# A gate pair's products in another order, and three moves of work in a hybrid state-space and attention block

## The chip, the cores and the metric

The kernel runs on one core of a Trainium2 chip. The metric is the device time of one execution in microseconds (us); a time of a kernel is the median of several executions. A profile is one more execution, recorded by the hardware profiler.

## What is computed

One block with 1024 frames and 1024 channels. An RMS norm of the input is modulated by a scale and a shift that come from a vector c, and one wide product of the result with `w_in` gives eight pieces:

```
mod = c @ w_ada[l] + b_ada[l]
shift, scale, gate = jnp.split(mod, 3, axis=-1)
h = _rmsnorm(x, g_pre[l]) * (1.0 + scale[:, None]) + shift[:, None]
proj = h @ w_in[l]
u_s, z_s, q_lat, kv_lat, k_rope, z_m, gl_s, gl_m = jnp.split(proj, split_at, axis=-1)
y_s = _ssm_branch(u_s, ...)          # 64 groups of 16 channels, 64 complex states each, a scan over frames
glu_a, glu_b = jnp.split(jax.nn.gelu(y_s) @ w_glu[l] + b_glu[l], 2, axis=-1)
y_s = ((glu_a * jax.nn.sigmoid(glu_b)) * jax.nn.silu(z_s)) @ w_br_ssm[l]
y_m = _mla_branch(q_lat, kv_lat, k_rope, ...)   # latent attention, 16 heads, rotary key
y_m = (y_m * jax.nn.silu(z_m)) @ w_br_mla[l]
merged = jax.nn.sigmoid(gl_s) * y_s + jax.nn.sigmoid(gl_m) * y_m
out = merged @ w_out[l]
x = x + gate[:, None] * _rmsnorm(out, g_post[l])
```

The four gates `z_s, z_m, gl_s, gl_m` are 32 tiles of 128 channels by 1024 frames.

## The kernel before

**Engines.** PE does the matrix products, DVE and POOL the elementwise work, ACT copies and functions, SP issues most of the transfers. Every engine runs its own instructions in one fixed order. For the part that the change touches, the code is written step by step and a scheduler sets each engine's order when the program is built, by its own estimate of times; the last part of the kernel is ordered by hand and isn't touched.

**Exact products.** A 32-bit product is made of three fast ones. A weight tile is split in halves of four blocks: ACT rounds it (`whi`, L113) and DVE subtracts (`wlo`, L114); four such pairs of buffers exist. A product over four blocks is 12 matmuls of 128x512.

**Head.** DVE makes the modulation in four quarters, `m` (L259 for the first of eight steps, L261 for seven more). PE sums a quarter (`mp`, L290) and transposes the normed input (`xtp`, L303), ACT makes `h`, and PE then makes the first three pieces u0 to u2 (`up`, L323). Beside that, DVE works on the layer's parameters: `exact_exp` for `dt` and `mag`, the angle `th`, the tables of powers and rotations (`rot`), all on small tiles. They go out to tables in DRAM, `tab_d` and `rot_d`, from which the state-space part reads.

**State-space blocks.** Eight blocks of two half blocks, numbered 0 to 15. For a half block, `ssm_wt` makes weights (`wt`, L809 to L811), `ssm_win` transposes them (`wps`, L819), and `ssm_turns` makes a table of turns: DVE computes `w` (L878 to L883), ACT writes it to `pk`, and four transfers bring it to `cs` (L891). `cs` and `pk` have one buffer each. `ssm_states` makes the inputs on PE (`xps`, L900) and the states on DVE (`z`, L915 to L922; L919 is the scan). `ssm_taps` makes `kps` on PE (L847), `kt` on ACT and DVE (L850), sends it through DRAM and back into `tt` by four transfers (L855). `ssm_y` needs `tt` and `z` (`yps`, L931).

**Gates.** In between, `next_gate(n)` hands out n units of other work for PE: first u3 to u7, then five plain tiles for the latents (four units each), then gate products, one unit each. `PER_SLOT` says how many at the three places of a block. Two gate tiles are a pair; its four quarters of outputs come from seven products by a scheme of Strassen and Winograd, each 12 matmuls. Their sums are made in `after` by DVE: five into `u` and the gate tiles `ga`, `gb` (L567, L605, L607, L612) and one more; `ga` and `gb` then go through ACT. Twelve pairs run in this way, four are deferred in part.

**Buffers.** Products land in PSUM tiles called `gp_`, each for two products (0 and 1, 2 and 3, 4 and 5, 6 alone); three such tiles exist. A tile is free when the last sum that reads it is done. Sums live in five buffers "ev" of 128x1024 that the whole part shares.

Of the kernel before, what the change touches and what calls it, by code (L numbers as in the profile page):

```python
# [8 lines left out]
F32 = mybir.dt.float32  # L9
# [17 lines left out]
NH = 16  # L27
L = 8

PER_SLOT = (5, 5, 4) * 8  # L30
AHEAD = 2
LAG = 4
ASIDE = 3
# [38 lines left out]
def _body(ctx, tc, a, out):  # L72
# [178 lines left out]
    def mod_quarter(n):  # L251

        m0 = xp.tile([128, 512], F32, name=f"m0{n}")
        for k in range(KT):
            wm = xp.tile([128, 512], F32, tag="wm", name="wm", bufs=8)
            wm_dma = nc.sync.dma_start(out=wm, in_=a["w_mod"][n, k])
            ck = cols[:, C_C + k:C_C + k + 1]
            if k == 0:
                V.tensor_scalar(m0, wm, ck, None, op0=ALU.mult)  # L259
            else:  # L260
                V.scalar_tensor_tensor(m0, wm, ck, m0, op0=ALU.mult, op1=ALU.add)  # L261
        macc.append(m0)
        return wm_dma

    for q in range(2):
        for t in range(4 * q, 4 * q + 4):
# [8 lines left out]
                V.tensor_scalar(xt[t], xt[t], r, None, op0=ALU.mult)  # L275
    first_w = []
    for n in range(4):
        wm_dma = mod_quarter(n)
        if n < 3:
            first_w.append(load_raw(a["w_in"][n]))  # L280
            if n < 2:
                first_w[n] = split_w(first_w[n])
# [65 lines left out]
    nc.sync.dma_start(out=dcol, in_=a["s_d"])  # L348
    lr, li = par[:, 1, :], par[:, 2, :]
    dt = tp.tile(GN, F32, name="dt")  # L350
    exact_exp(tp, dt, par[:, 0, :], GN, "dt")
    mag = tp.tile(GN, F32, name="mag")
    th = tp.tile(GN, F32, name="th")
    V.tensor_tensor(th, lr, dt, op=ALU.mult)
    exact_exp(tp, mag, th, GN, "mag")
    V.tensor_tensor(th, li, dt, op=ALU.mult)
    reduce_angle(tp, th, GN, "th")
    sn = tp.tile(GN, F32, name="sn")
    cs = tp.tile(GN, F32, name="cs")
    sin_cos(tp, sn, cs, th, GN, "th")  # L360

    pr = tp.tile([128, 9, G], F32, name="pr")
    pi = tp.tile([128, 9, G], F32, name="pi")
# [65 lines left out]
    fi = tp.tile(GN, F32, name="fi")  # L429
    den = tp.tile(GN, F32, name="den")  # L430
    nr = tp.tile(GN, F32, name="nr")
    V.tensor_tensor(den, lr, lr, op=ALU.mult)
    V.tensor_tensor(fr, li, li, op=ALU.mult)
    V.tensor_tensor(den, den, fr, op=ALU.add)
    V.reciprocal(den, den)
    V.tensor_scalar(nr, pr[:, 1, :], 1.0, None, op0=ALU.subtract)
    V.tensor_tensor(fr, nr, lr, op=ALU.mult)
    V.tensor_tensor(fi, pi[:, 1, :], li, op=ALU.mult)
# [114 lines left out]
    def gate_pair(p):  # L553
# [21 lines left out]
        def left(n):  # L575
            if n == 0:
                t["a"], t["b"] = load_raw(a["w_in"][8 + 2 * p]), load_raw(a["w_in"][9 + 2 * p])
                t["s"] = xp2.tile([128, KT, 128], F32, tag="sx", name="sx")
            a1, a2, b1, b2 = t["a"][:, 0:4], t["a"][:, 4:8], t["b"][:, 0:4], t["b"][:, 4:8]
            s1, s2 = t["s"][:, 0:4], t["s"][:, 4:8]  # L580
            if n == 0:
                P.tensor_tensor(s1, b1, b2, op=ALU.add)  # L582
                P.tensor_tensor(s2, s1, a1, op=ALU.subtract)
            if n == 2:
                P.tensor_tensor(a2, a2, s2, op=ALU.subtract)
            if n == 3:
                P.tensor_tensor(a1, a1, b1, op=ALU.subtract)
            return split_half((a1, a2, s2, s1, a2, a1, b2)[n])

        def product(n, w):  # L590
            if n % 2 == 0:
                t["p"] = ps.tile([128, S], F32, tag="A", name="gp_")
            t[n] = t["p"][:, HALF[n % 2]]
            quad_product(t[n], w, (0, 1, 2, 3, 5, 4, 6)[n])

        def after(n):
            if n == 0:
                t["u"], t["ga"] = ev("u"), ev("ga")
                A.activation(t["u"][:, HALF[0]], t[0], AF.Copy)
                return  # L600
            u1, u2 = t["u"][:, HALF[0]], t["u"][:, HALF[1]]
            if n == 1:
                add((t["ga"], 0), t[1], u1)
            elif n == 2:
                V.tensor_tensor(u2, t[2], u1, op=ALU.add)  # L605
            elif n == 3:
                V.tensor_tensor(u1, t[3], u2, op=ALU.add)  # L607
            elif n == 4:
                add((t["ga"], 1), t[4], u1)
                out_(t["ga"], p % 4 * 2)  # L610
            elif n == 5:
                V.tensor_tensor(u2, t[5], u2, op=ALU.add)  # L612
                t["gb"] = ev("gb")
                add((t["gb"], 1), t[3], u2)
            else:
                add((t["gb"], 0), t[6], u2)
                out_(t["gb"], p % 4 * 2 + 1)

        return left, product, after
# [124 lines left out]
    pos = tp.tile([128, 8], I32, name="pos")  # L744
    nc.sync.dma_start(out=pos, in_=a["pos"])
    posf = tp.tile([128, 8], F32, name="posf")
    V.tensor_copy(posf, pos)
    RS = [128, 8, 16]
    ang = tp.tile(RS, F32, name="ang")
    V.tensor_tensor(ang, posf.unsqueeze(2).to_broadcast(RS),  # L750
# [186 lines left out]
    u = ssm_load(0)  # L937
    wt = ssm_wt(0)
    turns = ssm_turns(0)
    next_gate(4)  # L940
    z = [ssm_states(0, ssm_win(wt), u[0], turns)]
    turns = ssm_turns(1)
    z.append(ssm_states(1, ssm_win(ssm_wt(1)), u[1], turns))
    turns = ssm_turns(2)
    ca = [ssm_ca(q) for q in range(2)]
    next_gate(4)
# [5 lines left out]
    for b in range(NB):  # L952
# [7 lines left out]
        spread()  # L960
        if more:
            z.append(ssm_states(2 * b + 2, ssm_win(wt), u[0], turns))
            wt = ssm_wt(2 * b + 3)
        spread()
        ssm_y(b, *this)
        if more:
            turns = ssm_turns(2 * b + 3)
            z.append(ssm_states(2 * b + 3, ssm_win(wt), u[1], turns))
            ca = [ssm_ca(2 * b + 2 + q) for q in range(2)]
            if b + 2 < NB:  # L970
                turns = ssm_turns(2 * b + 4)
# [993 lines left out]
```

## Time and profile before

| | |
|---|---|
| median of 3 executions | 1526.53 us (1525.48 to 1528.39) |
| the profiled execution | 1522.02 us, span 1520.2 us, mean granted clock 0.948 |
| head, to the end of the modulation sums | 0 to 60.9 us |
| u0 to u2 and on, tables made | 60.9 to 131 us |
| first five half blocks (z of half block 4 starts at its end) | 131 to 249.3 us |
| half blocks 4 to 14 (z to z) with gate pairs | 249.3 to 521 us |
| the last half blocks, to the operand of the latents' norm (`knrbdg`, L173) | 521 to 587 us |
| rotary, attention, output | 587 to 1520 us |

The stages overlap; the borders are single events read from the timeline. In rows of the timeline a figure in square brackets is idle time of that engine just before the instruction, with what ended it; x2 and so on is a count. A wait that the page calls "issue" was for nothing that the profile shows. The clock of PE is given as a share of 2.4 GHz.

### The profile page before, as it was taken

The numbers are of one execution on the slowest core, as the hardware profiler recorded it, in microseconds if no ns is written. First come the engines' busy times: TensorE is split into PE (matmuls) and PEld (weight loads), VectorE is DVE, ScalarE is ACT, GpSimd is POOL, SyncE is SP. The second block draws the span as 40 slices with busy tenths as digits, with TensorE's granted clock in tenths as the row PEclk, the third lists the DMA queues.
The fourth block names the chain that finished last, engine by engine and source line by source line (L and its number), as shares of the span: only waits on it lengthen the run. The fifth ranks groups of instructions, "written<-read, shape, count | busy, mean of one in ns | idle before, by whom it ended". The sixth has DMA issues, their size and how long they took to land. (4 is left out here: it accounts for less than half of the span.)

```text
span 1520.2 us, 19089 instructions
## 1 busy us (share of the span) xinstructions
PE 1335.6 (88%) x6172; PEld 1079.7 (71%) x6172; DVE 1203.1 (79%) x1917; ACT 765.6 (50%) x1374; POOL 595.9 (39%) x438
## 2 busy tenths in 40 slices
PE   3898988789889989977997999988999989989796
PEld 2686776668667767756876788866777767868574
DVE  5984799888989976896776877678777788787877
ACT  6522344344434334443756677756644465645553
POOL 1430564222423233453454434426033725556232
PEclk9899999899999999988998999989999999999999
DMA  8588555346435538674323321142278747873522
GB/s 321 208 156 215 177 167 174 108 127 180 132 121 154 149 108 282 229 268 144 114 85 139 115 64 53 36 118 84 81 221 263 234 146 277 289 264 122 188 72 97
DMA packets 154132, 246.34 MB, mean 162 GB/s; under 512 B 49824, under 2 KB 89632, under 8 KB 153520
## 3 DMA queue, kind: packets, MB, share of 16 engines
q1 hardware_dynamic: 147408, 224.14, 47.2%
q10 hardware_dynamic: 6336, 19.93, 3.4%
q8 instruction: 49, 0.80, 0.2%
q0 software_dynamic: 288, 1.05, 0.2%
q14 instruction: 51, 0.42, 0.1%
HBM read 161.97 MB, written 74.65 MB: 156 GB/s over the span
## 5 line engine op out<-in xcount | busy, mean ns | idle before, releaser
L1426 DVE TENSOR_TENSOR wlo<-lr,whi 128x512 fp32r<-128x512 f32 x137 | 93.9, 685 | 70.1 <-ACT lr L1423 69.8
L1196 POOL TENSOR_TENSOR plo<-p,phi 128x512 fp32r<-128x512 f32 x65 | 85.3, 1320 | 154.6 <-ACT phi L1194 119.2
L1188 ACT ACTIVATE p<-s_ps 128x512 f32<-128x512 f32 (+1 forms) x192 | 92.2, 488 | 64.2 <-DVE plo L1196 38.3
L114 DVE TENSOR_TENSOR wlo<-wraw,whi 128x512 fp32r<-128x512 f32 x110 | 97.0, 886 | 34.4 <-ACT whi L113 34.3
L113 ACT ACTIVATE whi<-wraw 128x512 fp32r<-128x512 f32 x110 | 68.3, 627 | 89.6 <-POOL wraw L667 11.2
L1196 DVE TENSOR_TENSOR plo<-p,phi 128x512 fp32r<-128x512 f32 (+3 forms) x127 | 81.0, 648 | 30.8 <-ACT phi L1194 30.2
L1194 ACT ACTIVATE phi<-p 128x512 fp32r<-128x512 f32 (+1 forms) x192 | 98.8, 525 | 4.1
L1538 PE MATMUL sw<-ge_hi,wlo 128*128 128x512 f32 x224 | 89.8, 401 | 6.7 <-DVE wlo L1426 6.7
L1538 PE MATMUL sw<-ge_hi,whi 128*128 128x512 f32 x224 | 88.5, 395 | 0.9 <-ACT oe L1213 0.7
L1538 PE MATMUL sw<-ge_lo,whi 128*128 128x512 f32 x224 | 88.2, 394 | 0.0
L1184 PE MATMUL s_ps<-q_hi,k_hi 128*128 128x512 f32 (+1 forms) x192 | 71.3, 372 | 12.8 <-DMA q_hi<-mr 11.0
L1419 ACT ACTIVATE whi<-raw 128x512 fp32r<-128x512 f32 x80 | 50.3, 629 | 61.5 <-PE sw L1538 42.5
L1211 PE MATMUL o_ps<-phi,v_hi 128*128 128x512 f32 (+1 forms) x192 | 69.4, 361 | 9.3 <-ACT phi L1194 9.1
L1211 PE MATMUL o_ps<-plo,v_hi 128*128 128x512 f32 (+1 forms) x192 | 66.9, 367 | 6.1 <-DVE plo L1196 5.1
L1184 PE MATMUL s_ps<-q_lo,k_hi 128*128 128x512 f32 (+1 forms) x192 | 69.1, 360 | 0.0
L1184 PE MATMUL s_ps<-q_hi,k_lo 128*128 128x512 f32 (+1 forms) x192 | 69.0, 360 | 0.0
L1211 PE MATMUL o_ps<-phi,v_lo 128*128 128x512 f32 (+1 forms) x192 | 67.6, 353 | 0.0
L1414 POOL TENSOR_TENSOR raw<-raw 128x512 f32<-128x512 f32 x16 | 22.8, 1427 | 102.9 <-DVE S L1409 60.8
L582 POOL TENSOR_TENSOR sx<-wraw 128x512 f32<-128x512 f32 x12 | 16.3, 1362 | 115.5 <-DMA wraw<-in_w_in 115.5
L1538 PEld LDWEIGHTS sw<-ge_hi,wlo 128*128 128x128 f32 x224 | 42.0, 188 | 21.8 <-DVE wlo L1426 12.5
L810 POOL TENSOR_TENSOR tm<-tab 128x512 f32<-128x512 f32 x16 | 22.6, 1414 | 87.2 <-DVE z L917 27.9
L1184 PEld LDWEIGHTS s_ps<-q_hi,k_hi 128*128 128x128 f32 x192 | 37.7, 196 | 21.1 <-issue 12.9
(1977 smaller groups left out, 4548.9 us busy)
## 6 DMA issues: line engine op xcount, KB each, us to landing
wraw<-in_w_in SPq DMA_DIRECT2D x53, 512.0 KB
wm<-in_w_mod SPq DMA_DIRECT2D x32, 256.0 KB
cs<-pk SPq DMA_DIRECT2D x64, 128.0 KB
raw<-in_w_glu SPq DMA_DIRECT2D x14, 512.0 KB
hq<-h_d SPq DMA_DIRECT2D x12, 512.0 KB
xt<-in_x SPq DMA_DIRECT2D x8, 512.0 KB
h_d<-hk SPq DMA_DIRECT2D x8, 512.0 KB
u_d<-ue SPq DMA_DIRECT2D x8, 512.0 KB
```

The source lines that it names most:

```text
L113: A.activation(hi, raw, AF.Copy)
L114: eng.tensor_tensor(lo, raw, hi.bitcast(F32), op=ALU.subtract)
L810: P.tensor_tensor(tm[:, :, 0:8, :], wi_.unsqueeze(3).to_broadcast(bc), bs_.unsqueeze(2).to_broadcast(bc), op=ALU.mult)
L1184: T.matmul(s_ps[:, 0:w], l[t][:, ks], r[t][:, qs:c1], start=(j == 0), stop=(j == 2))
L1188: lp["exp"] = A.activation(p32[:, o:w], s_ps[:, o:w], AF.Exp, scale=SCALE)
L1194: A.activation(phi[:, o:w], p32[:, o:w], AF.Copy)
L1196: eng.tensor_tensor(plo[:, o:w], p32[:, o:w], phi[:, o:w].bitcast(F32), op=ALU.subtract)
L1211: T.matmul(o_ps[half][:, c0:c0 + w], l[sl][:, kt, vs], r[:, 0:w], start=(kt == 0 and j == 0), stop=(last and j == 2))
L1414: P.tensor_tensor(src[4], a1, b1, op=ALU.subtract)
L1419: A.activation(hi, src[j], AF.Copy)
L1426: V.tensor_tensor(lo, x, hi.bitcast(F32), op=ALU.subtract)
L1538: T.matmul(p_, l[:, k, :], r[:, k, :], start=(k == 0 and i == 0), stop=(k == 3 and i == 2))
```

## The change

Four edits. (1) In a gate pair, the quarter products 3 and 4 of the scheme change places, so that `a1` less `b1` is the left side of the fourth product and `s1` of the fifth. The second sum of the products' tile 2 and 3 is then made after product 3, and `gb` is written for the first time after product 4 instead of 5. The number of splits, products and sums is the same. (2) The parameter steps on DVE (`exact_exp` twice, the angle, sine and cosine, `den`, `posf`) may only be issued after the last step of the modulation. (3) In the loop, `ssm_turns` of the odd half block is called ahead of its `ssm_wt` and not after `ssm_y`; ahead of the loop `ssm_wt(1)` gets its own line. (4) Eight units of other work ahead of the first half block's states where there were four, four more ahead of the second's, and one unit less in each of the eight blocks; the sum of units is the same.

```diff
-PER_SLOT = (5, 5, 4) * 8
+PER_SLOT = (5, 4, 4) * 8
...
-                V.scalar_tensor_tensor(m0, wm, ck, m0, op0=ALU.mult, op1=ALU.add)
+                last_m = V.scalar_tensor_tensor(m0, wm, ck, m0, op0=ALU.mult, op1=ALU.add)
...
-    exact_exp(tp, dt, par[:, 0, :], GN, "dt")
...
-    sin_cos(tp, sn, cs, th, GN, "th")
+    with tc.issue_after(last_m.ins):
+        exact_exp(tp, dt, par[:, 0, :], GN, "dt")
...
+        sin_cos(tp, sn, cs, th, GN, "th")
...
-            if n == 2:
+            if n == 1:
+                P.tensor_tensor(a1, a1, b1, op=ALU.subtract)
+            if n == 3:
                 P.tensor_tensor(a2, a2, s2, op=ALU.subtract)
-            if n == 3:
-                P.tensor_tensor(a1, a1, b1, op=ALU.subtract)
-            return split_half((a1, a2, s2, s1, a2, a1, b2)[n])
+            return split_half((a1, a2, s2, a1, s1, a2, b2)[n])
...
-            quad_product(t[n], w, (0, 1, 2, 3, 5, 4, 6)[n])
+            quad_product(t[n], w, (0, 1, 2, 4, 3, 5, 6)[n])
...
             elif n == 4:
-                add((t["ga"], 1), t[4], u1)
+                V.tensor_tensor(u2, t[4], u2, op=ALU.add)
+                t["gb"] = ev("gb")
+                add((t["gb"], 1), t[4], u1)
+            elif n == 5:
+                add((t["ga"], 1), t[5], u2)
                 out_(t["ga"], p % 4 * 2)
-            elif n == 5:
-                V.tensor_tensor(u2, t[5], u2, op=ALU.add)
-                t["gb"] = ev("gb")
-                add((t["gb"], 1), t[3], u2)
             else:
-                add((t["gb"], 0), t[6], u2)
+                add((t["gb"], 0), t[6], u1)
                 out_(t["gb"], p % 4 * 2 + 1)
...
-    next_gate(4)
+    next_gate(8)
     z = [ssm_states(0, ssm_win(wt), u[0], turns)]
     turns = ssm_turns(1)
-    z.append(ssm_states(1, ssm_win(ssm_wt(1)), u[1], turns))
+    wt = ssm_wt(1)
+    next_gate(4)
+    z.append(ssm_states(1, ssm_win(wt), u[1], turns))
...
             z.append(ssm_states(2 * b + 2, ssm_win(wt), u[0], turns))
+            turns = ssm_turns(2 * b + 3)
             wt = ssm_wt(2 * b + 3)
...
         if more:
-            turns = ssm_turns(2 * b + 3)
             z.append(ssm_states(2 * b + 3, ssm_win(wt), u[1], turns))
```

The scheduler then orders all engines anew up to the last part. Three places:

DVE in the head, the second quarter of the modulation (`m_261`) in the kernel before; names with `dt` and `den` are parameter steps:

```order
L259 TENSOR_SCALAR m_261<-wm,cols 128x512
L434 TENSOR_TENSOR den<-den,fr 128x64
L750 TENSOR_TENSOR ang<-posf,cols 128x128
L190 TENSOR_SCALAR dtk<-dtk 128x64
L261 SCALAR_TENSOR_TENSOR m_261<-wm,cols,m_261 128x512
L435 RECIPROCAL den<-den 128x64
L191 SCALAR_TENSOR_TENSOR dtr<-dtk,dtr 128x64
L261 SCALAR_TENSOR_TENSOR m_261<-wm,cols,m_261 128x512
```

And in the changed kernel, from the split of the first weights through quarters 2, 3 and 4:

```order
L114 TENSOR_TENSOR wlo<-wraw,whi 128x512 x4
L259 TENSOR_SCALAR m_261<-wm,cols 128x512
L261 SCALAR_TENSOR_TENSOR m_261<-wm,cols,m_261 128x512 x7
L259 TENSOR_SCALAR m_296<-wm,cols 128x512
L261 SCALAR_TENSOR_TENSOR m_296<-wm,cols,m_296 128x512 x7
L259 TENSOR_SCALAR m_323<-wm,cols 128x512
L261 SCALAR_TENSOR_TENSOR m_323<-wm,cols,m_323 128x512 x7
L187 TENSOR_SCALAR dtr<-par 128x64
L188 TENSOR_SCALAR dtm<-par 128x64
```

The parameter steps that stood between the steps of quarters 2 to 4 now all stand behind them; of these, 31 stood ahead of the end of quarter 3.

DVE from the last step of the turn table to the states of half block 12, before (`z_1139` is its state tile, `cs` its turns):

```order
L883 TENSOR_TENSOR w<-w 128x128
L850 SCALAR_TENSOR_TENSOR kt<-dcol,kt 128x16
L605 TENSOR_TENSOR u<-gp__3873,u 128x512
L114 TENSOR_TENSOR wlo<-wraw,whi 128x512
L607 TENSOR_TENSOR u<-gp__3873,u 128x512
L809 TENSOR_TENSOR wt<-tab 128x512
L114 TENSOR_TENSOR wlo<-wraw,whi 128x512
L567 TENSOR_TENSOR ga<-gp__3908,u 128x512
L612 TENSOR_TENSOR u<-gp__3908,u 128x512
L114 TENSOR_TENSOR wlo<-sx,whi 128x512
L567 TENSOR_TENSOR gb<-gp__3873,u 128x512
L915 TENSOR_TENSOR z_1139<-xps,cs 128x4x127
```

The same place in the changed kernel:

```order
L885 TENSOR_TENSOR w<-rot__3664 128x128
L886 TENSOR_TENSOR w<-w 128x128
L812 TENSOR_TENSOR wt<-tab 128x512
L853 SCALAR_TENSOR_TENSOR kt<-dcol,kt 128x16
L918 TENSOR_TENSOR z_1139<-xps,cs 128x4x127
L912 TENSOR_TENSOR t<-xps,cs 64x4x127
```

Ten operations stood between the table's last step and its first use for half block 12, and two do now. For the even half blocks 4, 6, 8, 10, 12 and 14 there stand 2, 2, 6, 5, 2 and 6 (before, from 6 on, 9 or 10); for the odd ones from 5 on 10 to 12 (before 4 to 7).

PE between `kps` and `yps` of block 4 (half blocks 8 and 9; `xps` here is of half block 10), before:

```order
L549 MATMUL gp__3500<-x_lo_1127,whi 128x512
L900 MATMUL xps<-u,win 128x128 x4
L549 MATMUL gp__3500<-x_hi_1126,whi 128x512
L549 MATMUL gp__3500<-x_hi_1126,wlo 128x512
L549 MATMUL gp__3500<-x_lo_1127,whi 128x512
...
L931 MATMUL yps<-u,tt_1131 128x128
```

And in the changed kernel, block 5 (both `kps` in one row, `xps` of half block 12):

```order
L850 MATMUL kps<-ca,bt 32x128 x8
L822 MATMUL wps<-ident,wt 128x128 x4
L903 MATMUL xps<-u,win 128x128 x4
L934 MATMUL yps<-u,tt_1131 128x128
L935 MATMUL yps<-z_1140,ca 128x128
```

Before, 39 matmuls of gate products stand between the second `kps` and `yps` in each of the last five blocks (8 ahead of `wps`, 22 ahead of `xps`, 9 behind it; in the last block all 39 at once); now there are none at two places in the loop and none in the last block, and 16 to 66 at the others.

Counts of the whole order: 128x512 matmuls that stand ahead of the first `wps` are 336 where they were 322, ahead of the first `xps` 363 (344), ahead of the `xps` of half block 4 759 (684), of half block 14 1536 (1455). Ahead of the norm's broadcast (`knrb`) they are 1680 in both. All sums of the gate pairs then stand ahead of the states of half block 15 on DVE or within three rows behind it, where 11 stood behind it before.

## Rows read from the trace of the kernel before

**Rows 1.** Windows by stage: length, busy us (count) by engine, PE clock, DMA.

```profile
0.00:60.90 60.90, 28.96 (x116) 22.81 (x116) 45.37 (x123) 32.07 (x54) 10.65 (x13) 0.92 0.80 290
60.90:131.00 70.10, 69.75 (x318) 57.38 (x318) 50.67 (x145) 24.00 (x38) 24.04 (x18) 0.98 0.82 189
131.00:249.30 118.30, 104.19 (x530) 86.15 (x531) 94.37 (x133) 45.57 (x78) 57.21 (x34) 0.94 0.52 159
249.30:521.00 271.70, 231.66 (x1130) 187.88 (x1129) 238.02 (x338) 107.39 (x178) 87.63 (x61) 0.92 0.48 144
521.00:587.00 66.00, 59.12 (x297) 48.74 (x296) 48.89 (x64) 25.79 (x40) 21.84 (x16) 0.95 0.50 161
```

**Rows 2.** Waits of PE, 0 to 720 us: total, times, longest, in us.

```profile
PE gp__2447 L549 <- DVE u L612: 8.8, 1, 8.8
...
PE yps L931 <- DMA tt<-kt_d: 7.0, 4, 3.3
PE wps L819 <- issue: 6.6, 1, 6.6
...
PE gp__2899 L549 <- DVE u L612: 3.6, 1, 3.6
```

**Rows 3.** Waits of DVE, 250 to 580 us.

```profile
DVE wlo L114 <- ACT whi L113: 12.7, 18, 1.8
DVE kt L850 <- ACT kt L849: 10.5, 5, 2.3
DVE z L915 <- DMA cs<-pk: 5.7, 3, 2.4
DVE ga L567 <- ACT u L599: 4.2, 7, 1.5
```

**Rows 4.** Timeline of the head, DVE and then PE: start, length.

```profile
39.48 0.19 DVE L197 TENSOR_SCALAR dtp<-dtp 128x64 f32<-128x64 f32 x1
39.70 0.23 DVE L196 TENSOR_TENSOR dtp<-dtp,dtr 128x64 f32<-128x64 f32 x1
...
39.62 1.05 PE L290 MATMUL mp<-ones,m 128*128 128x1 f32 x8 [2.20 <-DVE m L261]
...
48.58 1.84 PE L290 MATMUL mp<-ones,m 128*128 128x1 f32 x8 [3.82 <-DVE m L261]
```

**Rows 5.** Timeline, DVE, first weights of the state-space part.

```profile
133.89 0.69 DVE L809 TENSOR_TENSOR wt<-tab 128x512 f32<-128x512 f32 x1 [8.00 <-DMA tab<-tab_d]
```

**Rows 6.** Timeline around one wait of PE, DVE and then PE.

```profile
263.37 1.36 DVE L883 TENSOR_TENSOR w<-w 128x128 f32<-128x128 f32 x1
...
269.96 0.69 DVE L915 TENSOR_TENSOR z<-xps,cs 128x508 f32<-128x508 f32 x1 [2.42 <-DMA cs<-pk]
...
277.77 0.68 DVE L612 TENSOR_TENSOR u<-gp__2382,u 128x512 f32<-128x512 f32 x1
...
269.32 0.39 PE L549 MATMUL gp__2312<-h_lo,whi 128*128 128x512 f32 x1
278.50 0.79 PE L549 MATMUL gp__2447<-h_hi,whi 128*128 128x512 f32 x1 [8.79 <-DVE u L612]
```

**Rows 7.** Groups on DVE, 249 to 521 us: count, busy us, mean ns, idle before.

```profile
L114 DVE TENSOR_TENSOR wlo<-wraw,whi 128x512 fp32r<-128x512 f32 x46 | 38.9, 848 | 7.7 <-ACT whi L113 7.7
...
L518 DVE TENSOR_TENSOR h_lo<-hq,h_hi 128x512 fp32r<-128x512 f32 x4 | 3.1, 797 | 0.5 <-ACT h_hi L517 0.5
...
L567 DVE TENSOR_TENSOR ga<-gp__2724,u 128x512 f32<-128x512 f32 x1 | 1.1, 1134 | 1.3 <-ACT u L599 1.3
```

**Rows 8.** Timeline, the way from `kt` to `yps`: DVE, then PE.

```profile
244.54 0.66 DVE L850 SCALAR_TENSOR_TENSOR kt<-dcol,kt 128x16 f32<-128x16 f32 x1 [0.62 <-ACT kt L849]
...
253.24 0.75 PE L931 MATMUL yps<-u,tt 128*128 128x128 f32 x2 [3.31 <-DMA tt<-kt_d]
```

**Rows 9.** Timeline of PE in the last block: second `kps`, second half of `yps`.

```profile
565.01 0.43 PE L847 MATMUL kps<-ca,bt 128*32 128x128 f32 x8
...
578.58 0.49 PE L931 MATMUL yps<-u,tt 128*128 128x128 f32 x2 [0.94 <-DMA tt<-kt_d]
```

More of the change, by code (lines that the diff above doesn't have):

```diff
@@ L260, in mod_quarter @@
             else:
-                V.scalar_tensor_tensor(m0, wm, ck, m0, op0=ALU.mult, op1=ALU.add)
+                last_m = V.scalar_tensor_tensor(m0, wm, ck, m0, op0=ALU.mult, op1=ALU.add)
         macc.append(m0)
-        return wm_dma
+        return wm_dma, last_m
     for q in range(2):
@@ L277, in _body @@
     for n in range(4):
-        wm_dma = mod_quarter(n)
+        wm_dma, last_m = mod_quarter(n)
         if n < 3:
@@ L350, in _body @@
     dt = tp.tile(GN, F32, name="dt")
-    exact_exp(tp, dt, par[:, 0, :], GN, "dt")
[L352 to L359, printed above, removed]
-    sin_cos(tp, sn, cs, th, GN, "th")
+    with tc.issue_after(last_m.ins):
+        exact_exp(tp, dt, par[:, 0, :], GN, "dt")
+        mag = tp.tile(GN, F32, name="mag")
+        th = tp.tile(GN, F32, name="th")
+        V.tensor_tensor(th, lr, dt, op=ALU.mult)
+        exact_exp(tp, mag, th, GN, "mag")
+        V.tensor_tensor(th, li, dt, op=ALU.mult)
+        reduce_angle(tp, th, GN, "th")
+        sn = tp.tile(GN, F32, name="sn")
+        cs = tp.tile(GN, F32, name="cs")
+        sin_cos(tp, sn, cs, th, GN, "th")
     pr = tp.tile([128, 9, G], F32, name="pr")
@@ L431, in _body @@
     nr = tp.tile(GN, F32, name="nr")
[L432 to L435, printed above, removed]
+    with tc.issue_after(last_m.ins):
+        V.tensor_tensor(den, lr, lr, op=ALU.mult)
+        V.tensor_tensor(fr, li, li, op=ALU.mult)
+        V.tensor_tensor(den, den, fr, op=ALU.add)
+        V.reciprocal(den, den)
     V.tensor_scalar(nr, pr[:, 1, :], 1.0, None, op0=ALU.subtract)
@@ L746, in _body @@
     posf = tp.tile([128, 8], F32, name="posf")
-    V.tensor_copy(posf, pos)
+    with tc.issue_after(last_m.ins):
+        V.tensor_copy(posf, pos)
     RS = [128, 8, 16]
```

## The prediction

> **What bounds the kernel now.** I read the windows by stage first. From 587 us on nothing is changed in order, so the change must show before that. In the head PE is busy for 28.96 of 60.9 us and DVE for 45.37; from 60.9 to 131 us PE is full (69.75 of 70.1); from 131 to 249.3 us PE is busy 88% and DVE 80%; from 249.3 to 521 us DVE 88% and PE 85%; in the last 66 us PE 90% and DVE 74% [rows 1]. So the limits change: DVE and the modulation in the head, PE in the u pieces and the first half blocks, then DVE and PE in turns, DVE a little ahead.
>
> The waits of PE come next. One is for the first weights' transposes (6.6 us), four for `tt` (7.0), and six for the second sum of a gate pair, L612, from 8.8 down to 3.6 us; these six sum to 36.6 us [rows 2]. The last looks like the prize, so I looked at one closely. PE's last matmul of one pair ends at 269.7, and the next pair starts at 278.50, 0.05 us after L612 ends. In those nine us DVE stood only 2.42 us, for `cs`; the rest it worked [rows 6]. PE waits because DVE is behind, through a PSUM tile that comes free late. A tile that comes free sooner lets PE run ahead, but gives DVE no time. What it can give is the idle time of DVE that comes from PE or ACT being late: in the loop DVE is idle for 271.7 - 238.0 = 33.7 us [rows 1], and the waits behind it are for `whi` (12.7 us in 18 waits), `kt` (10.5), `cs` (5.7), and `u` of ACT (4.2) [rows 3].
>
> **Head, edit 2.** 31 small parameter steps stood ahead of the end of the modulation's quarter 3. One is 0.19 or 0.23 us long and the next follows after 0.22 [rows 4], others follow closer; at an estimated 0.15 that is 4.6 us that `m` gains. PE waits 2.20 us for quarter 2 and 3.82 us for quarter 3 [rows 4]; I take 5 of these 6.0 us, with bounds of 3 (0.10 a step) and 6.0. The steps are not saved: they run behind the modulation, on the same engine, under the u pieces' matmuls, and `mag` and all tables come as late as before. The tables come back from DRAM: DVE waits 8.0 us for the first of them, to 133.89 [rows 5], and PE 6.6 us for the transposes behind it [rows 2]. So the 5 us turn into a longer wait at this point unless something fills it.
>
> **First half blocks, edit 4.** 14 more matmuls stand ahead of the first `wps`, 19 ahead of the first `xps`, 75 ahead of that of half block 4. Where PE is full, from 60.9 to 131 us, 318 matmuls take 69.75 us, 0.22 us each [rows 1]; 75 are 16.5 us. PE's idle time from 131 to 249.3 us is 118.3 - 104.2 = 14.1 us [rows 1], and with the head's 5 there are 19.1 us to fill. I take it that they all fit: half block 4 starts its states at 249 as before, with a gate pair done that was not begun. Bounds: 3 us sooner (if the pair fits and a little idle time is left), 4 later (DVE has 17 operations more there; the stretch has 23.9 us without DVE work).
>
> **The loop, work.** From the states of half block 4 to those of 14, DVE has fewer operations than before: 4 splits of operands (L518), 3 sums into `ga` and `gb`, 3 into `u`, and one weight split more. By the group means of 0.80, 1.13 and 0.85 us and 0.68 us for a sum into `u` [rows 6, 7] this is 3.2 + 3.4 + 2.0 - 0.85 = 7.7 us less.
>
> **The loop, edit 3: the wait that it moves.** From the last `w` to `z` the transfers into `cs` need 269.96 - 263.37 = 6.6 us, the one case with a wait shown [rows 6]. In the new order the even half blocks 4 to 14 have 2, 2, 6, 5, 2 and 6 operations in that gap, worth 1.7, 1.5, 4.7, 4.1, 1.5 and 4.9 us by the same means (a split's 0.85 for `wt` too, 0.66 for `kt` [rows 8]): 18.4 of the 39.6 us that six such ways need, so 21.2 us of waiting. Five of these gaps hold a `kt`, whose wait for ACT, 10.5 us in five times, exists already [rows 3]; that leaves 10.7. The odd half blocks now have ten operations and more there, some 8 us, and their present waits for `cs` (5.7 us [rows 3]) go. Net 5.0 us more. Bounds: 0, if other waits shrink by as much while DVE stands, and 15.5, if `kt` hides nothing. What is queued behind the waiting `z` on DVE is the splits of weights and the pair's sums, so PE waits with it. On SP the table's four issues now stand among those of `kt` and `tt`; ways of 8.7 and 13.6 us from taps to `yps` exist already [rows 8, 9], and the 5 us between them are what SP's order can cost a block, up to DVE's queue behind it. POOL keeps its order here.
>
> The row says 6.6 us from `w` to `z`, for ACT's copies, four issues and the landing. The Trainium skill, DMA: Bandwidth & Descriptors, section "Anatomy of one DMA", states about 2 us fixed for a transfer, and its bytes at full rate (fitted on transfers that GpSimd issues). By an estimate from that page the way would be some 3 us, the new gaps of 4 us and more would hide it, and the loop would come out 5 us sooner. The measurement decides.
>
> **The loop, edit 1.** The tile of products 2 and 3 now comes free after product 3's sum, three products sooner, and PE can begin the next pair. What DVE can gain from it is part of its waits for ACT's `whi` and `u`, 12.7 + 4.2 us [rows 3], since ACT's splits wait for buffers that PE frees. I take a quarter, 4 us; the bounds are 0 and all 17. Against it stands that a pair now holds `ga` and `gb` together for two products longer, of five shared buffers; no wait for such a buffer shows now, so I set it at 0, and at most at one sum, 1.13 us [rows 7], in each of the twelve pairs, 13.6 us. The loop then moves by -7.7 + 5.0 - 4 = -6.7 us.
>
> **The end.** At half block 14, 81 more matmuls are done, worth 17.8 us by the 0.22 above, and DVE has 7 operations fewer behind it (6 weight splits and a sum, some 6.2 us). But `yps` now follows `kps` with nothing between. In the last block the second `kps` at 565.01 leads to the second half of `yps` at 578.58, 13.6 us, which 39 matmuls covered [rows 9]; the shortest such way is 8.7 us from `kt` [rows 8]. So PE cannot use its 17.8 us. I take DVE's saving less a small stall: -4 us, with bounds of -15 and +9.
>
> **Sum.** 0 - 6.7 - 4 = -10.7 us. Against the profiled execution, 1522.0, this is 1511.3; the runs' median is 4.5 us above that execution, so I forecast 1515.8, say **1516 us**.
>
> **Rivals.** (A) *The coupling was the bound.* PE's six waits of 36.6 us each let its clock fall: matmuls behind the one of 8.79 us start with 0.79 us where 0.39 is usual [rows 6]. If PE, ACT and DVE keep each other busy once the tile is free, DVE's idle time in the loop halves: -17 instead of +5.0 - 4. With -7.7 and -4 that is -28.7 us, 1498. For it: PE's waits are all of one kind. Against it: DVE worked through the wait that I looked at. (B) *Slower: the early table and the bare `yps`.* DVE pays the 15.5 us for `cs`, and in two blocks of the loop PE stands 8.7 to 13.6 us between `kps` and `yps` with no product to do. DVE has some 15 us of work queued there, so it runs dry for up to 5 us each, until PE has done 12 matmuls of the next product. 15.5 + 10 - 7.7 = +17.8 in the loop, with nothing from the end: 1544; half of that price, 9 us, gives 1535.5, which I take as its middle. It decides from the point where new waits outweigh the 7.7 us of work and the 4 at the end, at some 12 us, two for each even half block. For it: the order has the gap of one or two operations in it, and a queue is served in order. Against it: while DVE stands for `cs`, ACT and PE get ahead, and other waits shrink. (C) *It cancels.* The tables come no sooner, the head's gain is spent waiting for them, the loop's terms cancel: 1524 to 1529. That the order isn't changed is excluded, since the built order shows it.
>
> **How the numbers follow.** About 0.2% (3 us) is what a measurement of this kernel can tell from no change. My forecast case (1508 to 1523) has a chance of 0.40, A 0.15, B 0.28, C 0.17. Faster: 0.55, same 0.17, slower 0.28. The range holds the forecast case and C whole, A to about its middle and B to its middle: 1500 to 1537; the forecast's own range is 1508 to 1523.
>
> **What would show it.** Right: PE's waits for `m` under 1.5 us each; states of half block 4 near 249 us and of half block 14 near 515; waits of DVE for `cs` at even half blocks, 3 to 5 us each, and none at odd ones; the six waits of PE at L612 gone or a third, with waits for `tt` in their place; the norm's broadcast some 10 us sooner, and everything behind it by the same. Wrong: half block 4 later than 255 us, or DVE's idle time between half blocks 4 and 14 above 45 us (B) or under 20 us (A).

## The result, and the profile after

The changed kernel takes 1545.25 us (median of 4 executions, 1543.57 to 1548.34) where the kernel before takes 1526.01. The ratio is 1.0141, with a 95% interval of 1.0119 to 1.0163: slower by 1.4%, some 20 us, where I had forecast 10 us less. The profiled execution has a span of 1544.4 us, 24.2 longer than the one before.

The windows of the changed kernel, cut near the same events as [rows 1]: the last sums `mp` of the modulation (they start at 54.48 us, and at 60.99 before), the states of half block 4, those of half block 14, and the second of the norm's operands (`qnrbdg`). Columns are as there, and the stage up to 131 us is left out.

```profile
0.00:55.30 55.30, 27.31 (x124) 21.32 (x124) 39.26 (x65) 32.77 (x55) 11.38 (x13) 0.97 0.88 324
131.00:273.80 142.80, 128.47 (x629) 104.32 (x628) 108.90 (x149) 54.37 (x93) 63.93 (x39) 0.96 0.53 163
273.80:549.00 275.20, 234.31 (x1132) 191.09 (x1130) 230.61 (x328) 108.58 (x176) 87.54 (x60) 0.90 0.44 134
549.00:617.50 68.50, 50.27 (x229) 41.09 (x230) 46.32 (x61) 21.25 (x35) 22.61 (x16) 0.80 0.49 156
```

And the kernel before with its last border moved to the same `qnrbdg`:

```profile
521.00:592.10 71.10, 64.22 (x316) 52.30 (x315) 52.50 (x67) 28.03 (x44) 23.19 (x16) 0.95 0.54 174
```

So the difference of 24.2 us is made up of: 0.8 us up to the first states (146.25 and 145.45), 23.8 to half block 4 (273.83 and 249.26), 3.4 from there to half block 14 (275.20 and 271.78), -2.6 to `qnrbdg` (68.4 and 71.1), and -1.2 for all the rest. The first operand, `knrbdg`, at which the table of the kernel before ends, comes 51.9 us after half block 14 where it came 66.1 us after it. But the second now follows 16.5 us behind the first, where it was 5.0, and the rest keeps its length from the second.

Waits of PE in the loop from half block 4 to 14 (total, times, longest, in us):

```profile
PE yps L934 <- DMA tt<-kt_d: 16.6, 9, 4.3
PE wps L822 <- DVE wt L814: 7.7, 4, 2.4
PE kps L850 <- issue: 5.8, 1, 5.8
PE kps L850 <- DVE ca L842: 3.9, 4, 2.5
PE gp__2675 L551 <- DVE ga L569: 3.6, 1, 3.6
```

and of DVE there:

```profile
DVE wlo L114 <- ACT whi L113: 19.1, 12, 5.4
DVE z L918 <- DMA cs<-pk: 17.7, 5, 4.6
DVE kt L853 <- ACT kt L852: 4.8, 3, 3.4
```

The six waits of 36.6 us for a pair's second sum [rows 2] are gone. In their place PE waits for `tt`, for `ca` and for `wt`, all steps of the state-space part. DVE is idle for 275.2 - 230.6 = 44.6 us where it was 33.7; its waits for `cs` rose from 4.6 to 17.7 us (3.3 of these lie just ahead of half block 4's states, at the window's edge), and those for `whi` from 7.7 to 19.1. The clock of PE fell from 0.92 to 0.90 in the loop and from 0.95 to 0.80 behind it.

One of the two blocks of the loop with nothing between `kps` and `yps`, on PE (start, length, wait in brackets):

```profile
475.72 0.39 PE L551 MATMUL gp__4155<-h_lo,whi 128*128 128x512 f32 x1
476.36 0.43 PE L850 MATMUL kps<-ca,bt 128*32 128x128 f32 x8 [0.25 <-DVE ca L842]
482.56 0.65 PE L850 MATMUL kps<-ca,bt 128*32 128x128 f32 x8 [5.78 <-issue]
485.63 1.08 PE L822 MATMUL wps<-ident,wt 128*128 128x128 f32 x4 [2.42 <-DVE wt L814]
...
492.17 0.80 PE L934 MATMUL yps<-u,tt 128*128 128x128 f32 x2 [1.84 <-DMA tt<-kt_d]
```

on DVE:

```profile
480.64 1.81 DVE L842 TENSOR_TENSOR ca<-ca,tm 128x576 f32<-128x576 f32 x1
...
484.46 0.22 DVE L853 SCALAR_TENSOR_TENSOR kt<-dcol,kt 128x16 f32<-128x16 f32 x1
...
485.72 0.29 DVE L886 TENSOR_TENSOR w<-w 128x128 f32<-128x128 f32 x1
486.75 0.69 DVE L812 TENSOR_TENSOR wt<-tab 128x512 f32<-128x512 f32 x1 [0.74 <-PE wps L822]
487.36 0.23 DVE L853 SCALAR_TENSOR_TENSOR kt<-dcol,kt 128x16 f32<-128x16 f32 x1
491.71 0.69 DVE L918 TENSOR_TENSOR z<-xps,cs 128x508 f32<-128x508 f32 x1 [4.12 <-DMA cs<-pk]
```

and on SP's queue:

```profile
486.42 0.62 SPq L858 DMA_DIRECT2D tt<-kt_d  x1
487.15 2.57 SPq L894 DMA_DIRECT2D cs<-pk  x4
489.76 1.89 SPq L858 DMA_DIRECT2D tt<-kt_d  x3
```

From 476.1 to 498.8 us PE does the small matmuls of a block and no product at all. It waits for `ca` (the wait of the second `kps` row ends as L842 of 480.64 does), then for `wt`, then for `tt`, once more at 496.83 for 1.73 us. Meanwhile DVE comes to `z` and stands 4.12 us for `cs`. On SP the four issues of `cs` stand inside the four of the first `tt`. From 490.3 to 491.7 us both engines stand for a transfer, and what is queued behind on either has to wait with them.

The pause has a second price. In it the granted clock falls to 0.50, the lower of its two levels (1.2 of 2.4 GHz), and comes back to 1.00 only behind the next products:

```profile
482.50:498.80 16.30, 9.56 (x44) 7.98 (x45) 11.26 (x20) 4.13 (x8) 1.05 (x1) 0.50 0.42 106
498.80:502.80 4.00, 4.00 (x11) 3.15 (x11) 3.97 (x10) 0.32 (x1) 0.00 (x0) 0.50 0.06 18
502.80:515.00 12.20, 12.20 (x61) 10.23 (x60) 6.82 (x11) 10.27 (x14) 1.05 (x1) 1.00 0.56 193
```

### The profile page after: what moved, and what is told of

Read it like the earlier page. It is cut to its first block, busy times and chain, and to the rows that moved or that the text cites. A ratio compares the mean times of both kernels' runs of the same rounds, so it can differ in the third digit from the quotient of the medians.

```text
span 1544.4 us, 19098 instructions
## 1 busy us (share of the span) xinstructions
PE 1346.3 (87%) x6172; PEld 1088.2 (70%) x6172; DVE 1204.6 (78%) x1917; ACT 768.4 (50%) x1378; POOL 598.3 (39%) x438
## 5 line engine op out<-in xcount | busy, mean ns | idle before, releaser
L1201 DVE TENSOR_TENSOR plo<-p,phi 128x512 fp32r<-128x512 f32 (+3 forms) x127 | 77.1, 617 | 29.6 <-ACT phi L1199 29.1
L1189 PE MATMUL s_ps<-q_hi,k_hi 128*128 128x512 f32 (+1 forms) x192 | 72.0, 375 | 14.3 <-DMA q_hi<-mr 12.6
L934 PE MATMUL yps<-u,tt 128*128 128x128 f32 x128 | 36.0, 374 | 29.0 <-DMA tt<-kt_d 23.2
L1543 PEld LDWEIGHTS sw<-ge_hi,wlo 128*128 128x128 f32 x224 | 42.0, 187 | 20.7 <-DVE wlo L1431 11.4
```

Of the source, the lines that this page charges most:

```text
L934: T.matmul(yps[:, c], tt[q][:, i, :], u[q][:, i, :], start=True, stop=False)
L1189: T.matmul(s_ps[:, 0:w], l[t][:, ks], r[t][:, qs:c1], start=(j == 0), stop=(j == 2))
L1201: eng.tensor_tensor(plo[:, o:w], p32[:, o:w], phi[:, o:w].bitcast(F32), op=ALU.subtract)
L1543: T.matmul(p_, l[:, k, :], r[:, k, :], start=(k == 0 and i == 0), stop=(k == 3 and i == 2))
```

## The experiments

Eighteen runs. The table gives, from each profiled execution, the start of the states of half blocks 4 and 14, the time between them ("loop"), the time from half block 14 to `qnrbdg` ("end"), and the ratio on record to the kernel before in the same comparison (not quite the quotient of the two medians; the kernel before had medians of 1521.3 to 1526.6 us in these comparisons, so compare ratios). From `qnrbdg` to the end all take 922 to 932 us. A loop doesn't hold the same work in every kernel: it has 1108 (no_turns) to 1209 instructions of PE (no_fill), with 1130 before and 1132 in the changed kernel.

| kernel | half block 4 | loop | end | median | ratio (95%) |
|---|---|---|---|---|---|
| before | 249.3 | 271.8 | 71.1 | 1526 | 1 |
| all four edits | 273.8 | 275.2 | 68.4 | 1545 | 1.0141 (1.0119 to 1.0163) |
| edit 1, only_order | 249.2 | 257.9 | 68.5 | 1509.6 | 0.9885 (0.9841 to 0.9929) |
| edit 2, only_behind | 255.1 | 269.3 | 71.1 | 1526.8 | 1.0008 (0.9987 to 1.0029) |
| edit 3, only_turns | 250.8 | 271.7 | 69.0 | 1522.1 | 0.9986 (0.9959 to 1.0012) |
| edit 4, only_fill | 275.9 | 257.9 | 58.9 | 1522.6 | 0.9983 (0.9959 to 1.0007) |
| 2, 3, 4, no_order | 275.1 | 280.8 | 68.2 | 1548.4 | 1.0162 (1.0134 to 1.0189) |
| 1, 3, 4, no_behind | 277.1 | 273.2 | 65.5 | 1548.4 | 1.0165 (1.0135 to 1.0194) |
| 1, 2, 4, no_turns | 274.6 | 258.4 | 68.6 | 1531.6 | 1.0051 (1.0033 to 1.0070) |
| 1, 2, 3, no_fill | 257.1 | 275.4 | 74.8 | 1537.4 | 1.0097 (1.0063 to 1.0130) |
| 1, 2, order_behind | 253.3 | 264.2 | 67.2 | 1512.7 | 0.9927 (0.9900 to 0.9954) |
| 1, 3, order_turns | 252.0 | 271.0 | 64.2 | 1515.3 | 0.9957 (0.9937 to 0.9977) |
| 3, 4, turns_fill | 271.6 | 279.0 | 68.4 | 1550.3 | 1.0176 (1.0138 to 1.0215) |

**Each edit alone.** The edits are those of the diff ahead of the prediction, each by itself put into the kernel before.

only_order:

> Edit 1 alone (products 3 and 4 of a gate pair change places). The changed kernel lost its time before the states of half block 4 (24.6 of 24.2 us), where 75 more matmuls stood ahead of them. Theory 'front load': here 672 matmuls stand ahead of half block 4 (684 in the kernel before), so half block 4 stays within 3 us of 249 and the time within 4 us of the kernel before. Rival 'bare yps and cs': no gap of fewer than 4 operations between turn table and states, one block with no product between kps and yps: within 4 us too. Rival 'the tile that comes free sooner is a loss of its own, by the shared buffers held longer': 10 us or more slower, with waits in every block.

It is faster, by 1.2%, and a second comparison with five rounds, order_again, gave 1509.31 us and a ratio of 0.9898 (0.9874 to 0.9922). The loss of the changed kernel isn't edit 1's; none of the three theories had a gain.

> Edit 1 alone once more: 1508 to 1512 us, 0.8 to 1.2% under the kernel before. Nothing is left out.

The rows show where it comes from, waits of PE in its loop:

```profile
PE yps L931 <- DMA tt<-kt_d: 14.8, 10, 3.4
PE kps L847 <- DVE ca L839: 2.7, 3, 1.8
PE gp__2382 L549 <- ACT h_hi L517: 1.9, 2, 1.2
```

and of DVE:

```profile
DVE kt L850 <- ACT kt L849: 5.8, 4, 2.4
DVE z L915 <- DMA cs<-pk: 3.6, 3, 2.7
DVE wlo L114 <- ACT whi L113: 2.3, 3, 1.1
```

The 30.7 us of the loop's waits for L612 are gone, and only 15 for `tt` have come. The changed kernel waits hardly longer for `tt` (16.6 us) and is slower, so the sum of these waits does not tell the two apart. DVE's idle time in the loop is 257.9 - 233.6 = 24.3 us where it was 33.7.

only_behind:

> Edit 2 alone (layer parameters behind the modulation). All theories: the 5 us that PE gains in the head are given back at the first transposes, since the tables come no sooner: 0 to 3 us. If the head's gain reaches the end: 5 us faster. In the changed kernel PE's transposes of the rotary table then waited 4.9 us; if that is this edit's doing, the wait is here too.

No difference. PE's waits for `m` fall in the changed kernel as worked out (one of 1.78 us is left, the other is gone), and the gain is spent before the tables are there: PE waits 4.88 us for the rotary table's transposes, since the parameter steps that feed them now come later. With edit 2 alone the same wait is 4.39 us, so it is this edit's. The rows are of the changed kernel:

```profile
43.64 1.02 PE L290 MATMUL mp<-ones,m 128*128 128x1 f32 x8 [1.78 <-DVE m L261]
...
111.61 1.94 PE L771 MATMUL rtp<-ident,rtab 128*128 128x128 f32 x8 [4.88 <-DVE t L397]
138.52 0.63 PE L822 MATMUL wps<-ident,wt 128*128 128x128 f32 x4 [1.45 <-issue]
```

only_turns:

> Edit 3 alone (turn table of the odd half block sooner). Theory 'front load': 684 matmuls ahead of half block 4 as before, so within 4 us of the kernel before. Rival 'cs waits': the gaps between table and states hold 7 to 11 operations on this kernel's DVE, so no wait for cs above 2 us: within 4 us, or a gain of up to 6 us, since the waits for cs of before (5.7 us) go. If the edit by itself brings the loss: 10 us or more slower.

only_fill:

> Edit 4 alone (8 and 4 units ahead of the first two half blocks' states, one less in each block). Theory 'front load': 708 matmuls ahead of half block 4, 24 more than before and a third of the 75 of the changed kernel, so half block 4 some 8 us later and the time 5 to 10 us longer. Rival 'cs waits': even gaps of 5 to 9 operations, waits for cs of 5 us in all, 0 to 3 us. If the fill is free: within 3 us.

Neither is a difference that can be told from none. But only_fill is worth a look, since it took the theory of the front load away. Half block 4 is 26.6 us later, much more than the 8 that I had expected, and by `qnrbdg` it is all given back: 13.9 us in the loop and 12.2 at the end.

```profile
131.00:275.90 144.90, 124.37 (x569) 100.88 (x568) 106.10 (x145) 49.69 (x86) 63.33 (x39) 0.88 0.51 156
275.90:533.70 257.80, 231.70 (x1177) 187.93 (x1176) 226.88 (x334) 114.57 (x183) 86.82 (x60) 0.97 0.49 147
```

The end is shorter because less work is left for it (234 instructions of PE where there were 316). The loop isn't: PE has 1177 instructions there where it had 1130. But DVE has 226.88 us of work in the loop where it had 238.02, and the clock of PE is 0.97 where it was 0.92. Ahead of half block 4 it was the other way round, 0.88 and 0.94, so the clock has a likely part in the 26.6 us and in what came back.

**One edit taken out.** So the loss is in the company that the edits keep.

> The changed kernel without edit 1 (edits 2, 3, 4). Alone, edit 1 gained 17 us, edits 2 to 4 nothing each, all four together lost 19. Theory 'the fill and the early table collide': edits 3 and 4 together make the loss, so this is slow too, 1535 to 1550 us, with half block 4 at 270 or later and the way from half block 4 to 14 near 272 to 276 us. Rival 'edit 1 and the fill collide': without edit 1 nothing is lost, 1522 to 1530 us. Its order has even gaps of 4, 7, 5, 4, 4 and 5 operations and two blocks with nothing between kps and yps.

> The changed kernel without edit 2 (edits 1, 3, 4). Its order in the loop is nearly the changed kernel's. All theories: 1543 to 1548 us, within 4 us of it; if edit 2 has a part in the loss, 10 us or more less.

> The changed kernel without edit 3 (edits 1, 2, 4). Theory 'the fill and the early table collide': the loss goes, 1505 to 1520 us (edit 1's gain of 17 us, the fill free). Rival 'edit 1 and the fill collide': 1535 us or more, as 756 matmuls stand ahead of half block 4. Rival 'cs waits': its gaps between table and states are short for even and odd half blocks (3 to 8 operations), so waits for cs of 20 us and more and a time of 1530 us or more.

> The changed kernel without edit 4 (edits 1, 2, 3). Theory 'the fill and the early table collide', and 'edit 1 and the fill collide': 1505 to 1515 us, edit 1's gain is all there; half block 4 near 255 us (672 matmuls ahead of it). Rival 'edit 1 and the early table collide': 1530 us or more.

All four are slower than the kernel before. Edit 2 has no part in the loss as long as the other three are there (no_behind), and the loss needs no edit 1 (no_order). Taking edit 3 out gives 14 us back, all in the loop (275.2 to 258.4); taking edit 4 out gives 8. That no_turns is at 1531.6 and not near 1510 went against my theory. The rival 'cs waits' had the time, 1530 or more, but by waits for `cs` of 20 us and more, and there are 14.7. The loop of no_turns is as short as those of edits 1 and 4 alone, and its end is 10 us longer than that of edit 4 alone. no_fill at 1537.4 went against the theory too, and is what 'edit 1 and the early table collide' had; its loop is long with more work in it, 247.7 us of PE where there were 231.7.

**Pairs.**

> Edits 1 and 2 alone. Its order has 42 matmuls of gate products between kps and yps in every block from the third on and 7 to 10 operations between turn table and states. If these two things are what lets edit 1 gain: 1505 to 1513 us, as edit 1 alone or a little less. If edit 1's gain is lost with any other edit: 1522 us or more.

> Edits 3 and 4 alone; each alone is within 0.2% of the kernel before. Its order has 708 matmuls ahead of half block 4, even gaps of 5, 5, 4, 5, 3 and 5 operations, two blocks with nothing between kps and yps. Theory 'the two together make the loss': 1540 to 1550 us, as with edit 2 added. If the loss needs a third edit: 1522 to 1530 us.

> Edits 1 and 3 alone. Its order has 7 to 13 operations between turn table and states in every half block from the sixth on and 28 to 36 matmuls between kps and yps from the third block on, and no more work ahead of half block 4 than before. Theory 'gaps and cover decide': 1505 to 1515 us, as edit 1 alone. Rival 'edit 3 spoils edit 1 whatever the order': 1525 us or more.

Edits 3 and 4 are enough for the whole loss, 1550 us, though each is free alone. Edits 1 and 2 together keep most of the gain (1512.7). Edits 1 and 3 come to 1515.3, at the edge of what was expected: the order with gaps and cover isn't slow, but it has lost more than half of edit 1's gain, and I did not follow that up. It speaks against 'edit 1 and the early table collide', and then edit 2 is what parts it from no_fill: 1, 2 and 3 are at 1.0097 where 1 and 3 are at 0.9957. So edit 2, which does nothing alone or in the full set, costs 1.4% there, and no run tells why.

**The two ways replaced.** Five kernels tell what the wait for `tt` and that for `cs` are worth, by taking away what makes them wait. In the first, `tt` is loaded from a table that is written once, with zeros (the lines that set them are left out here and below):

```diff
+    kt_c = dram.tile([128, 2 * 128], F32, name="kt_c")
...
+    nc.sync.dma_start(out=kt_c, in_=kt.rearrange("q j p -> q (j p)"))
...
-                              in_=bass.AP(tensor=k_d.tensor, offset=k_d.offset + 32 * 256 * i + GP, ap=[[GP, 8], [256, GP], [1, 128]]))
+                              in_=bass.AP(tensor=kt_c.tensor, offset=kt_c.offset + 32 * 256 * i + GP, ap=[[GP, 8], [256, GP], [1, 128]]))
```

> The changed kernel, all four edits, but tt is loaded from a table in DRAM that is written once, so that yps no longer waits for the way from kps over kt; all other work and transfers stay (the output is not the reference's). PE's order stays nearly the same, three blocks have no product between kps and yps. In the changed kernel PE waited 16.6 us for tt between half blocks 4 and 14, and DVE 19.1 us for ACT's whi. Theory 'bare yps': both fall by more than half, the loop from 275 to about 260 us, the time to 1522 to 1532 us. Rival 'cs waits': DVE waits for cs instead, the loop stays within 5 us of 275 and the time is 1538 to 1546 us.

In the second, the four transfers into `cs` read such a table:

```diff
+    pk_c = [dram.tile([64, 2, 2, NC], F32, name=f"pk_c{i}") for i in range(2)]
...
-                nc.sync.dma_start(out=cs[o, :, g:g + 2, :], in_=pk[i])
+                nc.sync.dma_start(out=cs[o, :, g:g + 2, :], in_=pk_c[i])
```

> The changed kernel, all four edits, but the four transfers into cs read a table in DRAM that is written once, so that the states don't wait for w, ACT's copies and the landing; w and the copies are still made (the output is not the reference's). In the changed kernel DVE waited 17.7 us for cs in five times. Theory 'cs waits': the loop falls from 275 to about 260 us, the time to 1522 to 1532 us. Rival 'bare yps': PE still stands for tt, the loop stays within 5 us, 1538 to 1546 us. If each is half: 1532 to 1538 us.

Measured: taps_free 1526.0 us, ratio 1.0015 (0.9996 to 1.0035), loop 264.7, end 61.4; turns_free 1525.9 us, 1.0013 (0.9991 to 1.0034), loop 264.4, end 68.1. Each alone takes the whole loss away. That could not decide, so both together, and each on the kernel before:

> The changed kernel with both ways replaced: tt and cs come from tables in DRAM that are written once (the output is not the reference's). Each alone gave 1526 us, 19 less, with 10.5 us in the loop from half block 4 to 14. Theory 'two losses': the loop falls by some 21 us, to 254, and the time to 1505 to 1515 us. Rival 'one loss, either removal is enough': 1520 to 1528 us.

> The kernel before with tt from a table that is written once (the output is not the reference's). PE waited 7 us for tt there, and 39 matmuls covered most of the way. Theory 'the new order uncovers the ways': little here, 0 to 7 us, 1517 to 1526 us. Rival 'the way costs as much in any order': 15 us or more, under 1511 us, and then the 19 us of the changed kernel say nothing about the change.

> The kernel before with cs from a table that is written once (the output is not the reference's). DVE waited 5.7 us for cs there. Theory 'the new order uncovers the ways': 0 to 6 us, 1518 to 1526 us. Rival 'the way costs as much in any order': 15 us or more, under 1511 us.

| | kernel before | changed kernel |
|---|---|---|
| as it is | 1 | 1.0141 (1.0119 to 1.0163) |
| `tt` from a table | 0.9998 (0.9978 to 1.0018) | 1.0015 (0.9996 to 1.0035) |
| `cs` from a table | 0.9897 (0.9871 to 0.9923) | 1.0013 (0.9991 to 1.0034) |
| both | not run | 0.9937 (0.9912 to 0.9961) |

The medians are 1513.7 us for both_free, 1523.05 for taps_free_before and 1508.2 for turns_free_before, their loops 252.7, 270.8 and 260.3.

Each line is read across. As the kernels are, the change costs 1.4%; with `cs` from a table it still costs 1.2%; with `tt` from a table it costs 0.2%, which can't be told from none. So the second line of numbers is the answer. The way from the taps to `yps` is free in the kernel before, where 39 matmuls stand on it in five blocks, and costs 1.3%, 19 us, in the changed kernel. The zeros in the table are the same in both and gain nothing in the kernel before, so they aren't the reason. Between the two profiled executions, taps_free and the changed kernel, half block 4 is 2.4 us later, the loop 10.5 us shorter (275.2 and 264.7), the end 7.0 (68.4 and 61.4) and the unchanged rest 5.2, which is within what that rest differs by from run to run.

The way into `cs` costs 1.3% in the changed kernel but 1.0% in the kernel before too. The difference, some 4 us, is what came with the change, and by the intervals of the four ratios it can't be told from none. That this way costs 1.0% before went against my theory, by which it should have been worth 0 to 6 us there. Both ways together give 2.0%, less than the sum of 2.5; the 1513.7 us are inside what 'two losses' had.

Three limits. The rebuilt order moved a little with the new load: in taps_free 5, 4, 6, 4, 3 and 5 operations stand between table and states of the even half blocks. Then, the run prices the way and not the places that have no product on it: of the 16.6 us of waits for `tt` in the loop, 8.3 are at the two such places and 8.3 at places with 32 and 16 products. And with this way gone the change only breaks even, though edit 1 alone gains 1.1%. So a further loss of some 17 us against edit 1 alone is in the changed kernel, which no run here puts a name to.

The loop of taps_free shows that DVE's waits are in part the same loss, seen from another engine (waits of DVE from half block 4 to 14):

```profile
DVE wlo L114 <- ACT whi L113: 8.8, 9, 1.8
DVE z L921 <- DMA cs<-pk: 8.7, 3, 4.0
```

Those for `whi` fell from 19.1 to 8.8 us and those for `cs` from 17.7 to 8.7, though nothing but the little that moved in the order was done about either.

The same on edits 3 and 4 without edit 1:

> Edits 3 and 4, with tt from a table that is written once (the output is not the reference's). Theory 'the same loss': 15 to 20 us less than turns_fill (1550), 1528 to 1536 us. Rival 'without edit 1 the loss is another, of DVE and ACT': within 6 us, 1544 us or more. The order is not quite the same: even gaps of 8, 6, 6, 6, 4 and 5 operations where there were 5, 5, 4, 5, 3 and 5, worth up to 10 us, so a time between is no verdict.

It gave 1519.7 us, ratio 0.9978 (0.9961 to 0.9995), against 1550.3, a larger gain than the 15 to 20 us of 'the same loss'. So taking this way out takes the loss out there too, though the waits of PE for `tt` that the loop of turns_fill names sum to only 8.0 us. The order of this one moved more than the others': the place in the loop that had nothing between `kps` and `yps` now has 15 products, and the gaps are those of the expectation. So the 31 us are not all the way's.

## Why the prediction was wrong, step by step

**Head: right.** I took 5 us off PE's waits for `m` and said that they would be spent before the tables come. PE's sums of quarter 3 started 4.9 us sooner (43.64 and 48.58), and the first states 0.8 us later. The gain was gone earlier than I had it, in the 4.88 us for the rotary table, so it could not help the first half blocks.

**First half blocks: the step that failed first.** "I take it that they all fit": 75 more matmuls into PE's 14.1 idle us and the head's 5. In sum nothing fitted, and half block 4 came 24.6 us later. From 131 us to half block 4 PE was idle for 142.8 - 128.5 = 14.3 us, as much as before, and all the new work came on top: 24.3 us for 99 more instructions, where I had 16.5 for 75. PE's waits at the transposes of weights, which I meant to fill, fell from 11.5 us to 2.4, but others came up, the longest behind DVE, whose work there grew by 14.5 us. Waits of PE from 131 us to half block 4, the first two rows in the kernel before and the others in the changed one:

```profile
PE wps L819 <- issue: 6.6, 1, 6.6
PE wps L819 <- DVE wt L811: 4.9, 2, 3.7
PE yps L934 <- DVE qnv L148: 4.6, 1, 4.6
PE kps L850 <- issue: 3.7, 1, 3.7
PE wps L822 <- issue: 1.4, 1, 1.4
PE wps L822 <- DVE wt L814: 1.0, 1, 1.0
```

Still, in only_fill as much was given back later. In the changed kernel only 0.4 us of it was; in taps_free, with half block 4 as late, 23 us were.

**The loop, work: right.** I worked out 7.7 us less on DVE; its busy time fell by 7.4 (238.02 to 230.61).

**The loop, `cs`: right in kind, too small.** I had 10.7 us of new waits at the even half blocks and the present 5.7 gone, net 5.0. Five of six even half blocks wait, 2.2 to 4.6 us each, and no odd one. The total rose by 13.1 us, inside my bound of 15.5. For half block 4 the trace has four operations in the gap, not two, which makes my sum 1.7 us too high. By the runs with `cs` from a table the change is charged with only some 4 us of this. The estimate from the Trainium skill, DMA: Bandwidth & Descriptors, section "Anatomy of one DMA", was a way of some 3 us that gaps of 4 us and more would hide. The trace doesn't agree: with five operations in the gap, 4.1 us by my sum (half block 10), the states start 7.6 us after the table's last step and have waited 3.46 us, and with two (half block 12) 6.0 us after it (485.72 to 491.71).

```profile
428.41 0.28 DVE L886 TENSOR_TENSOR w<-w 128x128 f32<-128x128 f32 x1
436.02 0.69 DVE L918 TENSOR_TENSOR z<-xps,cs 128x508 f32<-128x508 f32 x1 [3.46 <-DMA cs<-pk]
```

**The loop, edit 1: wrong sign in this company.** I took 4 us off DVE's waits for `whi` and `u`. Waits for `whi` rose by 11.4 us. Alone, edit 1 does better than I thought: 13.9 us off the loop, most of it DVE's idle time, which falls from 33.7 to 24.3 us, its waits for `whi` from 7.7 to 2.3. My reading of the changed kernel is that PE stands at `yps` instead, the weight buffers are not freed, ACT's splits wait, and DVE waits for them; that the waits for `whi` are 8.8 us in taps_free fits it.

**The bare `yps`: the term that is missing from the sum.** I saw it in the order, priced it at nothing in the loop and at a small stall at the end, and at 10 us in rival B, since DVE has 15 us of work queued there. It is 19 us by the experiment with its control, of which the two profiled executions show 10.5 in the loop, as B had it, and 7.0 at the end. What the argument missed for the sum is that DVE's queued work is no help: in the block shown it holds the very steps (`ca`, `kt`, `w`) that the way consists of, and a wait for `cs`. It also took the stall for too short. I had PE between `kps` and `yps` for 8.7 to 13.6 us, and PE has no product for 22.7 us, since `kps` itself waits for `ca`. That front is not in the 19 us: with `tt` from a table the same block still has no product for 19.4 us, and PE waits no less ahead of `kps` in the loop (taps_free; the changed kernel has 5.8 and 3.9):

```profile
PE kps L853 <- issue: 11.5, 3, 6.2
```

**The end: right on balance.** -4 us was forecast and -2.6 measured. With `tt` from a table the end takes 61.4 us, so the uncovered way costs some 7 us there, where I had put a small stall of 2 (6.2 less 4).

**The rivals.** B named the waits that came, and its full price, 1544 us, is the time that came; I had put its middle at half and ended the range there. That the number fits is in part luck. `cs` was to pay most of it, and the uncovered `yps` did; and B had 17.8 us in the loop, which grew by 3.4, while it had nothing ahead of half block 4, where 24.6 came. A had the sign of edit 1 alone, but not the size: it halved DVE's idle time and came to 1498, and the run has 24.3 of 33.7 us left and 1509. Of my signs, half block 4 later than 255 us said wrong; DVE's idle time, 44.6, stayed just under the 45 of B.

**What stays open.** What takes edit 1's gain away in the changed kernel once the way to `tt` is out of it; why edits 1 and 3 keep less than half of that gain with gaps and cover in place, and lose 22 us more with edit 2; why no_turns loses 10 us at its end against only_fill; how much of turns_free_before's 1% is the wait itself and how much SP's queue, in which four issues for `cs` wait ahead of others.

## What to carry to other kernels

Before moving work ahead, look at what it covered where it was: here products stood between `kps` and `yps` while a way of some 8 us through DRAM ran (7.7 and 8.7 us from `kt` to `yps` in two places), and one table of credits and one call moved sooner, both free alone, took many of them away. When a rebuilt order shows an instruction directly behind the start of the transfer that it needs, price the whole way from the first operand of the pair, and count another engine's queued work as a bridge only if it isn't itself a part of the way. And put edits in one by one: the four edits alone sum to a gain of some 1.4%, and together they are as much slower; edit 1 alone, at 1509 us, beats both kernels.

## What was not expected of the hardware

A named wait is a poor price. With edit 1 alone PE's waits for `tt` sum to 14.8 us in the loop of a kernel that is 1.1% faster. In turns_fill they sum to 8.0 us, and taking the way away gained 31, with some of the order moved as well; in the kernel before, DVE's waits for `cs` sum to 5.7 us [rows 3], and taking that way away gained 1.0%, 15 us. Part of it is the clock: in the block shown above it stayed at 0.50 for 4 us of products behind the pause. How much of the whole that makes was not measured by itself. Over the loop of the changed kernel the clock was 0.90 of 2.4 GHz, and 0.94 in that of taps_free.

```profile
276.20:540.90 264.70, 228.65 (x1145) 187.57 (x1145) 233.44 (x329) 111.04 (x179) 91.48 (x60) 0.94 0.45 140
```

PE's busy time in the same loop is 228.65 us for 1145 instructions here and 234.31 for 1132 in the changed kernel.
